# Two transformer blocks on one core: half of the modulation rows on GpSimd, reciprocal roots on VectorE

## The chip, the core and the metric

The kernel runs as one program on one core of a Trainium2 chip. The metric is the time of one execution on the device in microseconds (us). The kernel before was run three times: 1963.08 us in the median, 1960.91 to 1964.33.

The core has five instruction streams: TensorE (PE in the rows; its weight loads are PEld), VectorE (DVE), ScalarE (ACT), GpSimd (POOL) and SyncE (SP, which here only issues DMAs). Each takes its own instructions strictly in order, and an instruction that waits holds up all behind it on its engine.

## The reference

256 rows of 2048 numbers go through two blocks. The part that the change touches is cut out here:

```
c_act = silu(c)                                     # one row of 2048
for l in range(2):                                  # block 1, two layers
    mod = c_act @ w_mod[l] + b_mod[l]               # 2048 x 6144 weights
    shift, scale, gate = split(mod, 3)
    h = rmsnorm(x, g) * (1 + scale) + shift
    ... h @ w_in -> attention over 64 chosen keys, retention, head norms ...
    x = x + gate * (y @ w_out[l])
... block 2: h @ w_in, gated convolution, a gated recurrence, w_o, a gate, a last rmsnorm ...
rmsnorm(x, g) = x * rsqrt(mean(x * x) + 1e-6) * g
```

The modulation is a product of one row with a large matrix; `rsqrt` stands in every norm.

## The kernel before, in words

**Weight groups.** Almost all of TensorE's work is in `wgroup`: 512 columns of a weight for both halves of the rows. A weight comes in chunks of two row blocks (512 KB, tile `raw`, issued by SyncE at L226, three buffers). ScalarE rounds a chunk to `whi` (L231), VectorE takes the rest `wlo` (L233), and TensorE runs three products for each row block and half (L249, L250, L251): 12 matmuls a chunk.

**Modulation sums.** `gemv` holds a sum `acc` of 128 x 1024 over 16 rows of `w_mod` per partition. Each row is a 512 KB load into `graw` (L347, SyncE, three buffers), and VectorE multiplies it with a number of `ct` and adds it to `acc` (L351 for the first row, L353 for the others). TensorE then sums `acc` over partitions (L361 for shift and scale, L385 for the gate). There are 12 such sums, six a layer. The first one, at the start, is the wide one: it uses `raw` buffers too, and nothing else runs beside it.

**Order.** The sums are generators that run in the background of the weight groups: after each chunk `step()` advances every job by its rate (`RATE`, such as 0.902 rows a chunk for the first layer's rows). A scheduler then orders each engine's instructions by program order, moved by the places in `AHEAD` (`gdve` puts the sum's rows ten places later). Layer 0 goes over its first ten groups in four passes of 20 chunks, each pass with a quarter of the rows of the weight. A pass needs the normed rows of its quarter, and so the modulation sum of that quarter, which runs in the pass before it.

**Reciprocal roots.** `rstd` turns sums of squares into reciprocal roots for 1, 2 or 4 columns, on GpSimd: L152 scales and adds the epsilon, L154 takes the power -0.5, L156, L157, L158 and L160 are one Newton step. It runs 33 times. Its results go to `dg` (L517, VectorE, at the start), to `rq` (L616), `nm` (L780) and `ev` (L600, L1097) on VectorE, to the rows of the next layer (L912, ScalarE) and to the last norm (L1283, L1285, L1287).

Of the kernel before, what the change touches and what calls it, by code (L numbers as in the profile page):

```python
# [18 lines left out]
P = 128  # L19
# [8 lines left out]
# steps of each background job per weight chunk  # L28
# [3 lines left out]
# places that instructions move forward in the order of issue  # L32
# [3 lines left out]
WJ, NB = 12, 6  # L36
# [3 lines left out]
def shape_constants():  # L40
    """Tables that depend on shapes alone."""
# [27 lines left out]
def build(tc, a, out):  # L69
# [4 lines left out]
    with es:  # L74
# [5 lines left out]
        # ---------------------------------------------------------------- helpers  # L80
# [20 lines left out]
        def step(n=1):  # L101
            """Advance every background job by its rate."""
# [12 lines left out]
        def spawn(gen, rate, then=None):  # L115
            """Start a background job; another may follow it."""
            bg.append([gen, rate, 0.0, then])
# [10 lines left out]
        def give(consumer, t, pt):  # L128
            """Run a consumer up to its yield; what follows waits for flush()."""
            r = consumer(t, pt)  # L130
            if r is not None:
                next(r)
                late.append(r)
# [15 lines left out]
        def rstd(ss, n, mean):  # L149
            """(ss * mean + EPS) ** -0.5 for a [P, n] tile of sums of squares."""  # L150
            v = sm(n, "rv")
            G.tensor_scalar(v, ss, mean, EPS, op0=OP.mult, op1=OP.add)  # L152
            y = sm(n, "ry")
            G.tensor_tensor(y, v, mhalf[:, 0:n], op=OP.pow)  # L154
            q = sm(n, "rq")
            G.tensor_mul(q, y, y)  # L156
            G.tensor_mul(q, q, v)  # L157
            G.tensor_scalar(q, q, -0.5, 1.5, op0=OP.mult, op1=OP.add)  # L158
            z = sm(n, "rz")
            G.tensor_mul(z, y, q)  # L160
            return z
# [6 lines left out]
        def split_ps(ps, gain=None):  # L168
            """A [P, 512] transposed block in PSUM into its two float32r parts."""
# [36 lines left out]
        def build_kg(src, kg, gains, shifts):  # L206
            """One tile of four transposed blocks: normed rows scaled, shifted, split."""
# [9 lines left out]
        def build_raw(src, kg, gains):  # L217
            """Four transposed blocks of rows that are still to be normed, times the norm's gains."""
            return split_ps(transpose4(src), gains[:, kg * 4:kg * 4 + 4])

        def wchunk(srcs, n, kt):
            """Two row blocks of a weight, loaded and split."""
# [13 lines left out]
        def wgroup(srcs, n, aT, kts, consumer, mode="k", tw=3):  # L236
            """out[t] = rows[t] @ W for one group of columns; kts are row blocks (pairs from even)."""
# [41 lines left out]
        # ---------------------------------------------------------------- constants, small vectors  # L279
# [9 lines left out]
        mhalf = con.tile([P, 4], F32, name="mhalf")  # L289
        G.memset(mhalf, -0.5)  # L290
# [35 lines left out]
        # ---------------------------------------------------------------- modulation  # L326
# [6 lines left out]
        def gemv(l, ranges, wide=False):  # L333
            acc = b1.tile([P, 1024], F32, name="acc", tag="acc", bufs=2)
            for j in range(16):
# [13 lines left out]
                with tc.high_priority(offset=AHEAD["gdve"]):  # L349
                    if j == 0:  # L350
                        V.tensor_scalar(acc, rf, ct[:, 0:1], None, op0=OP.mult)  # L351
                    else:
                        last[0] = V.scalar_tensor_tensor(acc, rf, ct[:, j:j + 1], acc, op0=OP.mult, op1=OP.add)  # L353
# [22 lines left out]
        def mod_gate(l, q):  # L376
            """Half q of layer l's gate, on every partition."""
# [16 lines left out]
        # ---------------------------------------------------------------- T5 bias table, rotary tables  # L394
# [82 lines left out]
        # ---------------------------------------------------------------- start  # L477
# [75 lines left out]
        # ---------------------------------------------------------------- block 1  # L553
        def from_ps(pt, sb):
            """Columns in SBUF: as they are, or copied out of PSUM."""
# [6 lines left out]
        def layer(l, hT, ap):  # L562
# [62 lines left out]
            def select(t):  # L625
                """0 where a key is among the TOPK of its row and not after it, NEG elsewhere."""
# [726 lines left out]
```

## Time and profile before

| | |
|---|---|
| median of three runs | 1963.08 us |
| the profiled execution, first to last instruction | 1964.1 us |
| TensorE busy | 1849.0 us (94%) |
| VectorE busy | 1313.3 us (67%) |
| ScalarE busy | 1044.1 us (53%) |
| GpSimd busy | 93.0 us (5%) |
| granted TensorE clock, mean | 0.986 |

The profiled execution's own time is given as its span. A row of a timeline reads: start, duration, engine, line, operation, tile written and tiles read, shapes, count, and in brackets how long the engine had been idle before it and what ended that. In a group of instructions, busy time and mean duration stand behind the first bar and idle time before them behind the second. TensorE's busy time is modelled from pipelined matmuls, so that a busy TensorE need not be at its peak.

### The profile page before, as it was taken

How to read it: one execution, taken by the hardware profiler on the slowest of the kernel's cores; microseconds unless marked ns; L12 is line 12 of the kernel's file. 1: busy time of each engine (PE TensorE's matmuls, PEld its weight loads, DVE VectorE, ACT ScalarE, POOL GpSimd, SP SyncE). 2: the span in 40 equal slices, each digit the busy share in tenths (PEclk: the TensorE clock that was granted, in tenths of full speed). 3: DMA queues.
4: the chain of work that ended last, by engine and by line, in shares of the span. 5: the costliest groups of instructions: out<-in, count | busy, mean ns of one | idle time of the engine just before them, and what ended most of it. 6: DMA issues, size and time to landing. Idle time of an engine off the chain costs nothing.

```text
span 1964.1 us, 24148 instructions
## 1 busy us (share of the span) xinstructions
PE 1849.0 (94%) x8670; PEld 1503.6 (77%) x8670; DVE 1313.3 (67%) x1713; ACT 1044.1 (53%) x1576; POOL 93.0 (5%) x220
## 2 busy tenths in 40 slices
PE   3988899998997999999999999999999999999997
PEld 3866577777776877688878878888888888888786
DVE  6787669998777677976755565656575545455554
ACT  3557484554435455447545675458445444445554
POOL 2000011001101002100000100000000000000100
PEclk9999899999998999999999999999999999999999
DMA  9987777987888898875547765556656666657564
GB/s 316 327 269 251 249 234 224 320 293 235 295 300 264 295 309 282 269 223 157 163 156 239 214 181 174 151 171 183 177 151 191 194 193 193 193 183 222 176 205 146
DMA packets 230921, 440.37 MB, mean 224 GB/s; under 512 B 19728, under 2 KB 32144, under 8 KB 230672
## 3 DMA queue, kind: packets, MB, share of 16 engines
q1 hardware_dynamic: 228880, 436.38, 70.5%
q10 hardware_dynamic: 1440, 2.34, 0.3%
q8 instruction: 68, 1.11, 0.2%
q14 instruction: 53, 0.43, 0.1%
q0 software_dynamic: 480, 0.10, 0.0%
HBM read 430.85 MB, written 7.91 MB: 223 GB/s over the span
## 4 chain that ended last, share of the span: by engine, by line
PE 60%; DMA 15%; DVE 11%; ACT 5%; issue 5%; POOL 3%; SPq 1%; ACTq 0%; DVEq 0%; POOLq 0%
PE mm L250 18%; PE mm L251 18%; PE mm L249 18%; DMA graw<-in_w_mod_dram 8%; DVE wlo L233 5%; DMA raw<-in_w_in_dram 4%; DMA rb<-reld 2%; ACT whi L231 2%; DVE acc L353 2%; PE tr L196 2%; PE tr L1070 1%; POOL ry L154 1%; DVE I L648 1%; POOL rv L152 1%; SPq L226 1%
## 5 line engine op out<-in xcount | busy, mean ns | idle before, releaser
L233 DVE TENSOR_TENSOR wlo<-raw,whi 128x1024 fp32r<-128x1024 f32 (+1 forms) x596 | 721.6, 1213 | 409.5 <-ACT whi L231 407.8
L231 ACT CAST whi<-raw 128x1024 fp32r<-128x1024 f32 (+1 forms) x596 | 621.9, 1045 | 696.7 <-PE mm L251 451.3
L250 PE MATMUL mm<-wlo,ah 128*128 128x512 f32 (+1 forms) x2368 | 935.8, 395 | 23.5 <-DVE wlo L233 23.2
L249 PE MATMUL mm<-whi,ah 128*128 128x512 f32 (+1 forms) x2368 | 934.5, 397 | 11.8 <-ACT ah L187 7.7
L251 PE MATMUL mm<-whi,al 128*128 128x512 f32 (+1 forms) x2368 | 931.0, 393 | 0.7 <-DVE al L188 0.6
L250 PEld LDWEIGHTS mm<-wlo,ah 128*128 128x128 f32 x2368 | 449.0, 190 | 132.2 <-DVE wlo L233 44.6
L249 PEld LDWEIGHTS mm<-whi,ah 128*128 128x128 f32 x2368 | 447.7, 189 | 108.8 <-ACT ah L187 8.4
L251 PEld LDWEIGHTS mm<-whi,al 128*128 128x128 f32 x2368 | 448.5, 189 | 92.1 <-DVE al L188 2.2
L353 DVE SCALAR_TENSOR_TENSOR acc<-graw,ct,acc 128x1024 f32<-128x1024 f32 x174 | 223.0, 1282 | 63.4 <-DMA graw<-in_w_mod_dram 62.8
L851 DVE TENSOR_TENSOR sp<-sp,mm 128x512 f32<-128x512 f32 (+1 forms) x64 | 42.0, 660 | 15.1 <-PE mm L251 15.0
L196 PE MATMUL tr<-blob,ev 128*128 128x128 f32 x192 | 34.2, 277 | 5.2 <-DVE ev L737 4.1
L179 ACT ACTIVATE ev<-tr,vT 128x128 f32<-128x128 f32 x112 | 32.4, 378 | 9.9 <-PE tr L196 9.3
L481 ACT ACTIVATE junk<-xs 128x512 bf16<-128x512 f32 (+1 forms) x42 | 25.6, 610 | 21.5 <-DMA xs<-in_x_dram 9.4
L152 POOL TENSOR_SCALAR rv<-tot 128x1 f32<-128x1 f32 (+1 forms) x9 | 3.7, 413 | 652.9 <-DVE tot L203 639.6
L154 POOL TENSOR_TENSOR ry<-rv,mhalf 128x4 f32<-128x4 f32 (+2 forms) x33 | 34.2, 1036 | 2.8
L196 PEld LDWEIGHTS tr<-blob,ev 128*128 128x128 f32 x192 | 23.6, 140 | 13.5 <-issue 6.0
L196 PE MATMUL tr<-blob,xs 128*128 128x128 f32 x128 | 24.5, 285 | 8.8 <-ACT xs L912 6.3
L462 ACT ACTIVATE oh<-rb,blob 128x512 f32<-128x512 uint8 x24 | 16.2, 715 | 27.0 <-DMA rb<-reld 27.0
L1070 PEld LDWEIGHTS tr<-X 128*128 128x128 f32 x224 | 27.0, 192 | 2.0 <-ACT uT L1119 1.0
L1070 PE MATMUL tr<-X 128*128 128x128 f32 x224 | 27.5, 276 | 0.1
L196 PEld LDWEIGHTS tr<-blob,xs 128*128 128x128 f32 x128 | 16.8, 146 | 13.8 <-ACT xs L912 7.4
L469 PE MATMUL ms<-ohr,rb 128*32 128x512 f32 x48 | 16.0, 428 | 11.2 <-ACT ohr L465 11.1
(275 smaller groups left out, 1183.8 us busy)
## 6 DMA issues: line engine op xcount, KB each, us to landing
raw<-in_w_in_dram SPq DMA_DIRECT2D x416, 512.0 KB
graw<-in_w_mod_dram SPq DMA_DIRECT2D x186, 512.0 KB
raw<-in_w_out_dram SPq DMA_DIRECT2D x64, 512.0 KB
raw<-in_w_o_dram SPq DMA_DIRECT2D x32, 512.0 KB
raw<-in_w_ple_gate_dram SPq DMA_DIRECT2D x32, 512.0 KB
raw<-in_w_a_out_dram SPq DMA_DIRECT2D x16, 512.0 KB
raw<-in_w_b_out_dram SPq DMA_DIRECT2D x16, 512.0 KB
raw<-in_w_in_dram SPq DMA_DIRECT2D x16, 256.0 KB
```

The source lines that it names most:

```text
L154: G.tensor_tensor(y, v, mhalf[:, 0:n], op=OP.pow)
L179: A.activation(e[:, s], ps[:, s], AF.Copy, scale=gain[:, i:i + 1])
L196: T.transpose(ps[:, s], src[:, s], ident)
L231: A.copy(hi, raw)
L233: V.tensor_sub(lo, raw, hi.bitcast(F32))
L249: T.matmul(o, ah, hi[:, j, :], start=first, stop=False)
L250: T.matmul(o, ah, lo[:, j, :], start=False, stop=False)
L251: T.matmul(o, al, hi[:, j, :], start=False, stop=end)
L353: last[0] = V.scalar_tensor_tensor(acc, rf, ct[:, j:j + 1], acc, op0=OP.mult, op1=OP.add)
L481: A.activation(junk[:, :n], src, AF.Square, accum_out=acc)
L851: V.tensor_add(h, h, pt[:, :n])
L1070: T.matmul(ps[:, h * P:(h + 1) * P], X[:, h, s], X[:, h, s], start=True, stop=True)
```

## The change

In every sum but the first, rows 8 to 15 go to GpSimd, as two instructions: the row is multiplied in its own buffer, and then added to `acc`. `NV = 8` is the row from which that holds. The reciprocal roots go to VectorE: an integer shift and subtraction on the bits of the number give a first guess, and three Newton steps of three instructions follow, 12 instructions in all in place of six. The tile `mhalf` goes. Loads, rates and places are as they were. Below, comments that were taken out and line moves are left out.

```diff
-WJ, NB = 12, 6
+WJ, NB, NV = 12, 6, 8
...
         def rstd(ss, n, mean):
             v = sm(n, "rv")
-            G.tensor_scalar(v, ss, mean, EPS, op0=OP.mult, op1=OP.add)
+            V.tensor_scalar(v, ss, mean, EPS, op0=OP.mult, op1=OP.add)
             y = sm(n, "ry")
-            G.tensor_tensor(y, v, mhalf[:, 0:n], op=OP.pow)
-            q = sm(n, "rq")
-            G.tensor_mul(q, y, y)
-            G.tensor_mul(q, q, v)
-            G.tensor_scalar(q, q, -0.5, 1.5, op0=OP.mult, op1=OP.add)
-            z = sm(n, "rz")
-            G.tensor_mul(z, y, q)
-            return z
+            V.tensor_scalar(y.bitcast(I32), v.bitcast(I32), 1, None, op0=OP.logical_shift_right)
+            V.tensor_scalar(y.bitcast(I32), y.bitcast(I32), -1.0, 1597463007.0, op0=OP.mult, op1=OP.add)
+            for _ in range(3):
+                q = sm(n, "rq")
+                V.scalar_tensor_tensor(q, y, -0.5, y, op0=OP.mult, op1=OP.mult)
+                V.tensor_mul(q, q, v)
+                z = sm(n, "rz")
+                V.scalar_tensor_tensor(z, q, 1.5, y, op0=OP.add, op1=OP.mult)
+                y = z
+            return y
...
                     if j == 0:
                         V.tensor_scalar(acc, rf, ct[:, 0:1], None, op0=OP.mult)
+                    elif wide or j < NV:
+                        last[0] = V.scalar_tensor_tensor(acc, rf, ct[:, j:j + 1], acc, op0=OP.mult, op1=OP.add)
                     else:
-                        last[0] = V.scalar_tensor_tensor(acc, rf, ct[:, j:j + 1], acc, op0=OP.mult, op1=OP.add)
+                        G.tensor_scalar(rf, rf, ct[:, j:j + 1], None, op0=OP.mult)
+                        last[0] = G.tensor_add(acc, acc, rf)
```

VectorE at the start, before the change: `tot` is the sum of squares of the input rows, `dg` the diagonal matrix with the reciprocal roots, and each `acc` a row of the first sum.

```order
L353 SCALAR_TENSOR_TENSOR acc<-raw,ct,acc 128x1024
L511 TENSOR_REDUCE tot<-sqx 128x2
L353 SCALAR_TENSOR_TENSOR acc<-graw,ct,acc 128x1024
L517 TENSOR_SCALAR dg<-blob,rz 128x128 x2
L353 SCALAR_TENSOR_TENSOR acc<-raw,ct,acc 128x1024
L353 SCALAR_TENSOR_TENSOR acc<-graw,ct,acc 128x1024
L353 SCALAR_TENSOR_TENSOR acc<-raw,ct,acc 128x1024
L353 SCALAR_TENSOR_TENSOR acc<-graw,ct,acc 128x1024 x4
```

The same place of the changed kernel, from the second `acc` behind `tot` on (`tot`, two steps, an `acc` and three more steps stand ahead of it).

```order
L355 SCALAR_TENSOR_TENSOR acc<-raw,ct,acc 128x1024
L162 SCALAR_TENSOR_TENSOR rz<-rq,ry 128x2
L159 SCALAR_TENSOR_TENSOR rq<-rz 128x2
L160 TENSOR_TENSOR rq<-rq,rv 128x2
L355 SCALAR_TENSOR_TENSOR acc<-graw,ct,acc 128x1024
L162 SCALAR_TENSOR_TENSOR rz<-rq,rz 128x2
L159 SCALAR_TENSOR_TENSOR rq<-rz 128x2
L160 TENSOR_TENSOR rq<-rq,rv 128x2
L355 SCALAR_TENSOR_TENSOR acc<-raw,ct,acc 128x1024
L162 SCALAR_TENSOR_TENSOR rz<-rq,rz 128x2
L522 TENSOR_SCALAR dg<-blob,rz 128x128 x2
L355 SCALAR_TENSOR_TENSOR acc<-graw,ct,acc 128x1024 x4
```

The steps of the reciprocal root stand between rows of the sum, and `dg` stands behind four rows of the sum where it stood behind one.

VectorE in the second half of the second sum, in layer 0's first pass, changed kernel: `wlo` is a weight chunk's rest, `Sh` what reads TensorE's sum of `acc`.

```order
L355 SCALAR_TENSOR_TENSOR acc<-graw,ct,acc 128x1024
L236 TENSOR_TENSOR wlo<-raw,whi 128x672
L355 SCALAR_TENSOR_TENSOR acc<-graw,ct,acc 128x1024
L236 TENSOR_TENSOR wlo<-raw,whi 128x1024 x2
L355 SCALAR_TENSOR_TENSOR acc<-graw,ct,acc 128x1024
L236 TENSOR_TENSOR wlo<-raw,whi 128x1024 x12
L368 TENSOR_TENSOR Sh_77<-tr,vT 128x4
```

Before, an `acc` stood between nearly every two of those last twelve; they are now on GpSimd, whose rows there are these (numbers tell the buffers apart).

```order
L357 TENSOR_SCALAR graw_521<-graw_521,ct_66 128x1024
L358 TENSOR_TENSOR acc_306<-acc_306,graw_521 128x1024
L357 TENSOR_SCALAR graw_543<-graw_543,ct_66 128x1024
L358 TENSOR_TENSOR acc_306<-acc_306,graw_543 128x1024
L357 TENSOR_SCALAR graw_571<-graw_571,ct_66 128x1024
L358 TENSOR_TENSOR acc_306<-acc_306,graw_571 128x1024
```

TensorE's sums of `acc` keep their places in its order in layer 0: behind chunk 18, 38 and 58 in both kernels.

VectorE where layer 0 ends, changed kernel: `tot` is the sum of squares of the new rows' first half, `xs` those rows.

```order
L206 TENSOR_REDUCE tot<-ssx 128x1
L355 SCALAR_TENSOR_TENSOR acc<-graw,ct,acc 128x1024
L236 TENSOR_TENSOR wlo<-raw,whi 128x1024 x2
L153 TENSOR_SCALAR rv<-tot 128x1
L892 TENSOR_TENSOR xs<-mm,gate 128x512
L155 TENSOR_SCALAR ry<-rv 128x1
L355 SCALAR_TENSOR_TENSOR acc<-graw,ct,acc 128x1024
L156 TENSOR_SCALAR ry<-ry 128x1
L159 SCALAR_TENSOR_TENSOR rq<-ry 128x1
L160 TENSOR_TENSOR rq<-rq,rv 128x1
```

Before, the same `acc`, `wlo`, `xs` and `acc` followed `tot`, but the reciprocal root ran beside them on GpSimd.

## Rows read from the trace of the kernel before

**Rows 1.** The page: span, and busy time of each engine.

```profile
span 1964.1 us, 24148 instructions
PE 1849.0 (94%) x8670; PEld 1503.6 (77%) x8670; DVE 1313.3 (67%) x1713; ACT 1044.1 (53%) x1576; POOL 93.0 (5%) x220
```

**Rows 2.** Busy time by stage: us; PE, PEld, DVE, ACT, POOL; clock, DMA, GB/s.

```profile
45.00:98.00 53.00, 53.00 (x244) 44.20 (x244) 41.32 (x42) 29.28 (x42) 0.00 (x0) 0.98 0.97 329
98.00:295.00 197.00, 171.35 (x744) 127.96 (x743) 141.34 (x182) 128.66 (x218) 9.14 (x22) 0.95 0.78 250
295.00:835.00 540.00, 502.67 (x2380) 401.30 (x2380) 437.96 (x627) 267.25 (x447) 41.66 (x89) 0.98 0.85 281
835.00:1964.00 1129.00, 1108.34 (x5220) 917.67 (x5219) 666.26 (x829) 601.10 (x837) 31.30 (x84) 0.99 0.61 184
```

**Rows 3.** The page's groups: weight rests, their matmuls, the sums' rows.

```profile
L233 DVE TENSOR_TENSOR wlo<-raw,whi 128x1024 fp32r<-128x1024 f32 (+1 forms) x596 | 721.6, 1213 | 409.5 <-ACT whi L231 407.8
L250 PE MATMUL mm<-wlo,ah 128*128 128x512 f32 (+1 forms) x2368 | 935.8, 395 | 23.5 <-DVE wlo L233 23.2
L353 DVE SCALAR_TENSOR_TENSOR acc<-graw,ct,acc 128x1024 f32<-128x1024 f32 x174 | 223.0, 1282 | 63.4 <-DMA graw<-in_w_mod_dram 62.8
```

**Rows 4.** Timeline at the start: the diagonal, the transposes, the first sum's matmuls.

```profile
26.47 0.48 DVE L517 TENSOR_SCALAR dg<-blob,rz 128x128 f32<-128x128 f32 x2 [2.00 <-POOL rz L160]
26.81 9.14 PE L198 MATMUL tr<-dg,xs 128*128 128x128 f32 x64 [11.09 <-DVE dg L517]
37.55 0.69 PE L361 MATMUL tr<-blob,acc 128*128 128x1 f32 x5 [1.60 <-DVE rbd L441]
```

**Rows 5.** Timeline: GpSimd instructions that begin beside a VectorE instruction, in pairs.

```profile
105.36 1.27 DVE L353 SCALAR_TENSOR_TENSOR acc<-graw,ct,acc 128x1024 f32<-128x1024 f32 x1
105.52 1.59 POOL L415 TENSOR_TENSOR tmp<-pti,tmp 128x256 int32<-128x256 int32 x1 [0.90 <-DVE tmp L417]
...
301.38 1.28 DVE L353 SCALAR_TENSOR_TENSOR acc<-graw,ct,acc 128x1024 f32<-128x1024 f32 x1
301.52 1.46 POOL L152 TENSOR_SCALAR rv<-ssq 128x4 f32<-128x4 f32 x1 [4.83 <-ACT junk L481]
```

**Rows 6.** Timeline: a VectorE instruction that begins beside a GpSimd one.

```profile
294.51 1.01 POOL L154 TENSOR_TENSOR ry<-rv,mhalf 128x4 f32<-128x4 f32 x1
294.55 1.23 DVE L233 TENSOR_TENSOR wlo<-raw,whi 128x1024 fp32r<-128x1024 f32 x1
```

**Rows 7.** Timeline: second sum's row 8; TensorE at the second and fourth sums' ends.

```profile
69.38 1.28 DVE L353 SCALAR_TENSOR_TENSOR acc<-graw,ct,acc 128x1024 f32<-128x1024 f32 x1
...
92.78 1.84 PE L361 MATMUL tr<-blob,acc 128*128 128x1 f32 x16
...
245.44 1.80 PE L361 MATMUL tr<-blob,acc 128*128 128x1 f32 x15 [1.17 <-DVE acc L353]
```

**Rows 8.** Timeline where layer 0 ends.

```profile
589.90 0.15 DVE L203 TENSOR_REDUCE tot<-ssx 128x1 f32<-128x4 f32 x1
593.61 0.69 DVE L887 TENSOR_TENSOR xs<-mm,gate 128x512 f32<-128x512 f32 x1
594.10 0.19 POOL L160 TENSOR_TENSOR rz<-ry,rq 128x1 f32<-128x1 f32 x1
595.10 1.97 PE L196 MATMUL tr<-blob,xs 128*128 128x128 f32 x8 [4.80 <-ACT xs L912]
```

**Rows 9.** VectorE's smallest operation by form, and waits for reciprocal roots (us, times, longest).

```profile
L366 DVE SCALAR_TENSOR_TENSOR Gm<-mq,vT 128x4 f32<-128x4 f32 x8 | 1.3, 160 | 0.1
DVE nm L780 <- POOL rz L160: 13.2, 8, 2.3
DVE ev L1097 <- POOL rz L160: 12.7, 4, 3.6
DVE rq L616 <- POOL rz L160: 10.2, 7, 2.3
```

**Rows 10.** Timeline at the end: the last norm's first use.

```profile
1958.08 0.49 DVE L1285 TENSOR_SCALAR xs<-xs,rz 128x512 f32<-128x512 f32 x1 [2.04 <-POOL rz L160]
```

More of the change, by code (lines that the diff above doesn't have):

```diff
@@ L287, in build @@
         lev = con.tile([P, 7, P], U8, name="lev")
-        mhalf = con.tile([P, 4], F32, name="mhalf")
-        G.memset(mhalf, -0.5)
         vT = con.tile([P, 128], F32, name="vT")
```

## The prediction

> **What bounds the kernel now.** The page says TensorE first: it is busy for 1849.0 of 1964.1 us [rows 1]. The table by stage then says where it is not. From 835 us on it idles for 20.7 of 1129 us, so nothing that the change does to another engine can be worth much there. Before that it idles for 62.98 us (25.65 from 98 to 295, 37.33 from 295 to 835), in stages where the DMAs are busy for 0.78 to 0.97 of the time and VectorE for 620.6 of 790 us [rows 2]. All 12 modulation sums lie in this first part. The groups say how VectorE and TensorE meet there: the second of a chunk's three matmuls idles for 23.5 us in all, almost only for `wlo`, and the sums' rows keep VectorE for 223.0 us and leave it idle for 63.4 us more while it waits, in order, for their loads [rows 3]. So the change can win at most about what TensorE waits for `wlo`, and can lose wherever a sum or a reciprocal root that TensorE waits for comes later.
>
> **The rows that go to GpSimd.** 11 sums by 8 rows: 88 multiply-adds of 1.282 us leave VectorE, 112.8 us, and with them about half of the 63.4 us of waiting in its queue [rows 3]. In place of each GpSimd runs two instructions over 1024 columns. The trace has none so wide. The widest on GpSimd is the int32 subtraction of 256 columns: it began at 105.52, beside a VectorE row of a sum that ended at 106.63, and ended at 107.11, 0.48 us later [rows 5]. By columns that is 1.92 us for 1024, 3.8 us for a row of a sum, and this I take. From below: the 4-column `rv` ended 0.32 us after the VectorE instruction beside it (301.38 + 1.28 to 302.98), so 252 more columns cost 0.16 us, and 1024 columns 0.32 + 0.65 = 0.97 us, 1.9 a row. From above: the whole 1.59 us as GpSimd's own price is 6.4 us, 12.7 a row. The nearest row is the subtraction's own part.
>
> *Does GpSimd run beside VectorE?* Both pairs of [rows 5] say that it waits: a 4-column `rv` lasts 1.46 us when it begins 0.14 us into a sum's row, and the end of that row ends it. The other way round, `wlo` began 0.04 us into a GpSimd power of 1.01 us and took 1.23, against 1.213 on average [rows 3, 6]; but that power reads four columns. The Trainium skill (SBUF — State Buffer, Who interferes with whom) says that a VectorE instruction with two SBUF inputs and a GpSimd instruction that reads SBUF share a port as an exclusive lock, held by whichever began first for its whole length. The rows agree for the one direction; no row here shows it for the other, which would speak against this change. The skill's GPSIMD Engine Reference (Elementwise — side-by-side cycle accounting) gives 4497 ns for an addition of 2048 columns; an estimate from that page is 2.25 us for 1024, which would make the row 4.2 us in place of 3.8.
>
> *The second sum.* Layer 0's first pass is bound by TensorE (53.00 of 53 us [rows 2]). 244 matmuls at 12 a chunk are 20.3 chunks, 2.6 us each. Row 8 was added at 69.38; the new order lets SyncE issue its load two chunks earlier, so GpSimd can begin near 64.2, and eight rows of 3.8 us end at 94.6. TensorE came to the sum at 92.78 without idle time [rows 7]: +2 us. With rows of 1.9 us it is 0; with two waits of 1.22 us for `wlo` in each row (6.2 us) it is +21 us. Behind the waiting matmul stand the whole next pass, and on VectorE `Sh` and all that follows it.
>
> *The fourth sum.* There TensorE already idles for 1.17 us for the last row [rows 7]. A last row of 3.8 us in place of 1.28 adds 2.5 us (0.6 to 5). The third sum's rows came 4 us apart and the later sums end well ahead of their matmuls: 0.
>
> *What VectorE loses.* If GpSimd's instructions also hold VectorE, 88 rows of 3.8 us are 334 us. VectorE's slack in 45 to 835 is 790 - 620.6 = 169 us, and 112.8 are freed: 52 us too much is the upper end. The lower end is 0, as in [rows 6]. I take 6, near the row, since that row is of a short reader.
>
> *What TensorE gains.* Of its 23.5 us for `wlo` all could go at best; GpSimd rows are under half of all rows of the sums, so I take -10.
>
> **The reciprocal roots.** 12 instructions of 0.16 us [rows 9] are 1.9 us, as long as VectorE's wait for GpSimd at the end (2.04 [rows 10]): the end costs 0. 33 times 12 are 396 instructions or 63 us of VectorE, and 36.1 us of waits for `rz` go [rows 9]: 27 us more, spread over stages where VectorE has 632 us to spare: 0, covered by that slack; without it a few us (bounds -4 and +5).
>
> Two places lose, because a chain that ran beside VectorE's queue now stands in it. *Start:* `dg` moves behind three more rows of the first sum (3 x 1.28) and 12 steps (1.9), and the 2.00 us of waiting goes: +3.8 us. The transposes then end at 26.81 + 9.14 + 3.8 = 39.75, and with ScalarE's last copy of some 0.6 the sum's matmuls begin at 40.35, not 37.55: +2.8 us (1 to 5) [rows 4]. *End of layer 0:* from `tot` (589.90) to `rz` (594.29) it took GpSimd 4.4 us, and TensorE idled for 4.80 us for what follows. Now an `acc` (1.28), two `wlo` (2.4), `xs` (0.69), another `acc` (1.28) and 12 steps (1.9) stand in VectorE's queue ahead of the result: 7.6 us, +3.2 (0 to 3.5) [rows 3, 8].
>
> **Sum.** +2.8 + 2 + 2.5 + 3.2 + 6 - 10 = +6.5 on the profiled span of 1964.1, so 1970.6; that span lies 1.0 above the median of the runs, which makes the forecast 1970 us.
>
> **Rivals.**
> *Relief wins.* VectorE no longer stands waiting for half of the loads, `wlo` comes in time, and SyncE gets `raw` buffers back sooner. For it: the 63.4 us of waits in VectorE's own queue, and 23.5 on TensorE. Against it: the DMAs are at 0.85 and more in those stages already. With all of the 23.5, no holding of VectorE, short GpSimd rows (second sum 0, fourth +0.6) and the two lost places (+6): -17, 1946 us. It decides where GpSimd's row stays under the 2.6 to 4 us in which rows arrive.
>
> *They cancel.* Relief of 15, VectorE not held, the sums' ends as forecast: +2.8 + 2 + 2.5 + 3.2 - 15 = -4.5, or somewhat less relief: 1963 us.
>
> *The two engines take turns.* A GpSimd instruction holds VectorE as VectorE holds GpSimd. Place: rows 8 to 15 of each sum. Price: a GpSimd row takes 6.2 us, the second sum ends 21 us late, and `wlo` is held for some of the 52 us. With half of that: +2.8 + 21 + 5 + 3.2 + 26 - 10 = +48, less what the loads gain while TensorE stands, say 15: 1996 us. It decides when a GpSimd row takes more than 4 us. The Trainium skill's exclusive lock (SBUF — State Buffer) would do this.
>
> **Chances.** Slower as forecast 0.31, taking turns 0.12, relief 0.36, cancelling 0.21. 0.2% of 1963 us, 3.9 us, is what a measurement tells from no change: faster by more 0.36, within 0.21, slower by more 0.43. The likeliest case alone runs from 1965 to 1982. The range for 8 in 10 goes from 1943 to 1997: from all of the relief to the turns.
>
> **What would show it.** GpSimd's busy time by its two new lines: near 88 x 3.8 = 334 us. TensorE's idle time before the second and the fourth sum's matmuls: 2 and 3.7 us. `dg` near 30 us, the first weight matmul near 46 in place of 43.3. The mean `wlo` beside GpSimd rows: 1.21 if it isn't held, above 1.5 if it is. TensorE's wait for `wlo`: 13 us in place of 23. I am wrong if GpSimd's row takes under 2.5 us, or if the `wlo` waits vanish whole.

## The result, and the profile after

The changed kernel took 2148.65 us (median of 4 runs, 2144.98 to 2156.88), the kernel before 1962.24 us (4 runs, 1960.91 to 1964.33): a ratio of 1.0955, 95% interval 1.093 to 1.098. The forecast of 1970 us, range 1943 to 1997, was far too low: the sign was right, the size was not.

The page of the changed kernel, to be held against [rows 1]:

```profile
span 2143.2 us, 24433 instructions
PE 1897.2 (89%) x8670; PEld 1539.3 (72%) x8670; DVE 1375.0 (64%) x2021; ACT 1044.7 (49%) x1576; POOL 529.1 (25%) x197
...
PE 57%; POOL 17%; DMA 9%; DVE 9%; issue 3%; ACT 3%; SPq 0%; ACTq 0%; DVEq 0%; POOLq 0%
```

The third line is the chain of work that ended last. GpSimd, busy for a quarter of the time, is 17% of it, some 364 us. Before the change it was 3%:

```profile
PE 60%; DMA 15%; DVE 11%; ACT 5%; issue 5%; POOL 3%; SPq 1%; ACTq 0%; DVEq 0%; POOLq 0%
```

The span is 179.1 us longer: TensorE idles for 246.0 us in place of 115.1 (span less busy), and is busy for 48.2 us more with the same 8670 matmuls. The table by stage (us; PE, PEld, DVE, ACT, POOL; clock, DMA, GB/s) says where, with the stages of [rows 2] moved by the delay:

```profile
45.00:112.00 67.00, 53.73 (x216) 42.51 (x216) 34.62 (x30) 28.99 (x41) 44.07 (x15) 0.88 0.73 245
112.00:350.00 238.00, 185.13 (x784) 139.54 (x785) 136.31 (x207) 133.04 (x228) 97.08 (x36) 0.90 0.66 214
350.00:1010.00 660.00, 532.44 (x2346) 423.65 (x2345) 492.20 (x750) 265.25 (x440) 379.98 (x128) 0.90 0.70 229
1010.00:2143.00 1133.00, 1113.84 (x5245) 922.47 (x5243) 684.91 (x989) 602.16 (x839) 0.00 (x0) 0.99 0.61 183
```

The last stage, without sums, takes 1133 us against 1129 before. All the rest arises where the sums are. There the DMAs, at 0.78 to 0.97 before, are down to 0.66 to 0.73, and the mean granted clock is 0.88 to 0.90 (a mean over TensorE's two levels, 1.2 and 2.4 GHz) in place of 0.95 to 0.98: the 48.2 us more of "busy" are matmuls at the lower level, in stretches with gaps. Less traffic and more idle time fit weights that come late.

The groups that answer to [rows 3], the two new GpSimd lines, and the matmuls at the sums' ends:

```profile
L236 DVE TENSOR_TENSOR wlo<-raw,whi 128x1024 fp32r<-128x1024 f32 (+1 forms) x596 | 764.1, 1284 | 503.3 <-ACT whi L234 501.6
L253 PE MATMUL mm<-wlo,ah 128*128 128x512 f32 (+1 forms) x2368 | 947.7, 400 | 51.2 <-DVE wlo L236 51.0
L357 POOL TENSOR_SCALAR graw<-graw,ct 128x1024 f32<-128x1024 f32 x88 | 298.8, 3396 | 385.8 <-DMA graw<-in_w_mod_dram 217.9
L358 POOL TENSOR_TENSOR acc<-acc,graw 128x1024 f32<-128x1024 f32 x88 | 222.7, 2530 | 32.2 <-DVE acc L355 25.0
L355 DVE SCALAR_TENSOR_TENSOR acc<-graw,ct,acc 128x1024 f32<-128x1024 f32 x86 | 118.8, 1382 | 39.5 <-DMA graw<-in_w_mod_dram 38.9
L366 PE MATMUL tr<-blob,acc 128*128 128x1 f32 x128 | 21.4, 297 | 33.5 <-POOL acc L358 33.5
```

A GpSimd row is 3.40 + 2.53 = 5.9 us, not 3.8. VectorE's `wlo` went from 1.213 to 1.284 us, and TensorE's wait for it from 23.2 to 51.0 us. But these waits do not add up to 131 us. The missing view is SyncE's own queue, whose waits nothing counts as busy (us in all, times, longest):

```profile
SPq L229 <- DVE wlo L236: 1036.6, 455, 13.6
SPq L349 <- POOL acc L358: 285.1, 68, 7.5
```

The first is the normal state of a queue that runs ahead until a weight buffer comes free (1104.3 us before the change). The second is new. Before the change SyncE waited for VectorE's rows, for 58.4 us in all and never longer than 3.8:

```profile
SPq L347 <- DVE acc L353: 58.4, 49, 3.8
```

How the two meet is seen in the second half of the second sum. GpSimd's timeline (start, us, and so on):

```profile
84.55 2.41 POOL L358 TENSOR_TENSOR acc<-acc,graw 128x1024 f32<-128x1024 f32 x1
86.94 3.91 POOL L357 TENSOR_SCALAR graw<-graw,ct 128x1024 f32<-128x1024 f32 x1
90.94 2.35 POOL L358 TENSOR_TENSOR acc<-acc,graw 128x1024 f32<-128x1024 f32 x1
93.26 3.82 POOL L357 TENSOR_SCALAR graw<-graw,ct 128x1024 f32<-128x1024 f32 x1
97.16 2.35 POOL L358 TENSOR_TENSOR acc<-acc,graw 128x1024 f32<-128x1024 f32 x1
```

and SyncE's:

```profile
86.99 0.37 SPq L349 DMA_DIRECT2D graw<-in_w_mod_dram  x1
87.46 0.41 SPq L229 DMA_DIRECT2D raw<-in_w_in_dram  x1
93.31 0.37 SPq L349 DMA_DIRECT2D graw<-in_w_mod_dram  x1
93.77 0.42 SPq L229 DMA_DIRECT2D raw<-in_w_in_dram  x1
99.54 0.37 SPq L349 DMA_DIRECT2D graw<-in_w_mod_dram  x1
```

GpSimd's addition ends at 86.96, and at 86.99 SyncE issues the load into the buffer that this frees; only then, in order, the load of one weight chunk at 87.46. The next pair comes with the next addition, 6.3 us later. The weight buffer had long been free: with three buffers, the chunk three places earlier had to be done, and VectorE's `wlo` of that one ended at 81.75. TensorE then waited 2.16 us for the chunk that was loaded at 87.46:

```profile
79.59 2.16 DVE L236 TENSOR_TENSOR wlo<-raw,whi 128x1024 fp32r<-128x1024 f32 x1 [2.06 <-ACT whi L234]
...
93.14 0.50 PE L252 MATMUL mm<-whi,ah 128*128 128x512 f32 x1 [2.16 <-ACT whi L234]
```

Before the change TensorE used up a chunk in 2.6 us; from 81 to 100 us it now gets one for each of GpSimd's rows.

### The profile page after: what moved, and what is told of

It is laid out like the page before. It is cut to its first block, busy times and chain, and to the rows that moved or that the text cites. A ratio compares the mean times of both kernels' runs of the same rounds, so it can differ in the third digit from the quotient of the medians.

```text
span 2143.2 us, 24433 instructions
## 1 busy us (share of the span) xinstructions
PE 1897.2 (89%) x8670; PEld 1539.3 (72%) x8670; DVE 1375.0 (64%) x2021; ACT 1044.7 (49%) x1576; POOL 529.1 (25%) x197
## 3 DMA queue, kind: packets, MB, share of 16 engines
q10 hardware_dynamic: 1440, 2.34, 0.3%
## 4 chain that ended last, share of the span: by engine, by line
PE 57%; POOL 17%; DMA 9%; DVE 9%; issue 3%; ACT 3%; SPq 0%; ACTq 0%; DVEq 0%; POOLq 0%
PE mm L253 17%; PE mm L254 17%; PE mm L252 17%; POOL graw L357 10%; POOL acc L358 7%; DMA graw<-in_w_mod_dram 5%; DVE wlo L236 3%; DVE acc L355 1%; DMA raw<-in_w_out_dram 1%; PE tr L199 1%; PE tr L1075 1%; ACT whi L234 1%; DMA raw<-in_w_in_dram 1%; DVE I L653 1%; PE tr L366 1%
## 5 line engine op out<-in xcount | busy, mean ns | idle before, releaser
L236 DVE TENSOR_TENSOR wlo<-raw,whi 128x1024 fp32r<-128x1024 f32 (+1 forms) x596 | 764.1, 1284 | 503.3 <-ACT whi L234 501.6
L253 PE MATMUL mm<-wlo,ah 128*128 128x512 f32 (+1 forms) x2368 | 947.7, 400 | 51.2 <-DVE wlo L236 51.0
L252 PE MATMUL mm<-whi,ah 128*128 128x512 f32 (+1 forms) x2368 | 949.9, 403 | 22.4 <-ACT whi L234 14.0
L254 PE MATMUL mm<-whi,al 128*128 128x512 f32 (+1 forms) x2368 | 941.4, 398 | 11.0 <-DVE al L191 10.9
L254 PEld LDWEIGHTS mm<-whi,al 128*128 128x128 f32 x2368 | 455.5, 192 | 106.1 <-DVE al L191 13.3
L357 POOL TENSOR_SCALAR graw<-graw,ct 128x1024 f32<-128x1024 f32 x88 | 298.8, 3396 | 385.8 <-DMA graw<-in_w_mod_dram 217.9
L358 POOL TENSOR_TENSOR acc<-acc,graw 128x1024 f32<-128x1024 f32 x88 | 222.7, 2530 | 32.2 <-DVE acc L355 25.0
L355 DVE SCALAR_TENSOR_TENSOR acc<-graw,ct,acc 128x1024 f32<-128x1024 f32 x86 | 118.8, 1382 | 39.5 <-DMA graw<-in_w_mod_dram 38.9
L366 PE MATMUL tr<-blob,acc 128*128 128x1 f32 x128 | 21.4, 297 | 33.5 <-POOL acc L358 33.5
L366 PEld LDWEIGHTS tr<-blob,acc 128*128 128x128 f32 x128 | 21.4, 258 | 35.4 <-POOL acc L358 35.0
L182 ACT ACTIVATE ev<-tr,vT 128x128 f32<-128x128 f32 x112 | 32.7, 375 | 13.4 <-PE tr L199 10.9
L653 DVE SCALAR_TENSOR_TENSOR I<-sc,wi,I 128x128 f32<-128x128 f32 (+1 forms) x60 | 36.2, 604 | 0.5
L353 DVE TENSOR_SCALAR acc<-graw,ct 128x1024 f32<-128x1024 f32 x12 | 16.0, 1332 | 30.7 <-DMA graw<-in_w_mod_dram 30.7
```

What stands on the lines that cost most here:

```text
L236: V.tensor_sub(lo, raw, hi.bitcast(F32))
L252: T.matmul(o, ah, hi[:, j, :], start=first, stop=False)
L253: T.matmul(o, ah, lo[:, j, :], start=False, stop=False)
L254: T.matmul(o, al, hi[:, j, :], start=False, stop=end)
L357: G.tensor_scalar(rf, rf, ct[:, j:j + 1], None, op0=OP.mult)
L358: last[0] = G.tensor_add(acc, acc, rf)
```

## The experiments

All times are medians of 4 to 10 runs, beside runs of the kernel before of 1964.36 to 1965.91 us. The two theories through most of them: *pace* (SyncE stops for GpSimd's buffers, with the weights behind), and *hold* (GpSimd's instructions keep VectorE's waiting).

**The two halves of the change.** The roots alone:

```diff
-WJ, NB, NV = 12, 6, 8
+WJ, NB, NV = 12, 6, 16
```

> All rows of the sums on VectorE again, reciprocal roots on VectorE as in the changed kernel. Theory P (the pace of a GpSimd row, 5.9 us against the 3 to 5 us in which rows come, is what costs: it keeps the three row buffers, SyncE waits for them, and the weights behind them come late): the 186 us go, and what is left is the two places named in the prediction, +6 us: 1968 us (1962 to 1974). Theory R (the 12 steps in VectorE's queue cost): over 2000 us.

Measured: 1976.01 us, ratio 1.006 (1.0046 to 1.0075). The rows alone, with the roots of before:

```diff
-            V.tensor_scalar(v, ss, mean, EPS, op0=OP.mult, op1=OP.add)
+            G.tensor_scalar(v, ss, mean, EPS, op0=OP.mult, op1=OP.add)
             y = sm(n, "ry")
+            G.tensor_tensor(y, v, mhalf[:, 0:n], op=OP.pow)
...
```

> Half of the rows on GpSimd, reciprocal roots on GpSimd as before the change. Theory P: the loss stays, and the roots now queue behind rows of 5.9 us: 2140 to 2200 us. Theory R: most of the loss goes, under 2000 us.

Measured: 2152.23 us, 1.0955 (1.0928 to 1.0982). The rows are all of the loss; the roots cost 12 us alone and can't be seen beside the rows.

**Which of the roots.** VectorE keeps the roots of four columns; those of one or two go back to GpSimd:

```diff
         def rstd(ss, n, mean):
+            if n < 4:
+                v = sm(n, "rv")
+                G.tensor_scalar(v, ss, mean, EPS, op0=OP.mult, op1=OP.add)
+                y = sm(n, "ry")
+                G.tensor_tensor(y, v, mhalf[:, 0:n], op=OP.pow)
...
+                return z
             v = sm(n, "rv")
...
```

> All rows on VectorE, and of the roots only those of four columns (the heads' norms) on VectorE; those of one or two columns (the rows' norms, at the start and at the ends of the layers, and the key's) on GpSimd as before. Theory P (the 12 us that the roots alone cost arise where a row's root stands between two products with nothing to cover it, and VectorE works off its twelve small instructions among long ones): 1955-1968 us. Rival Q (they arise at the heads' roots, which make the block's streams of long VectorE work later): 1970-1980 us.

Measured: 1964.03 us, 0.9992 (0.9971 to 1.0013): no change from before. The 12 us of the roots are those of the rows' norms (and the key's, which went back with them). The heads' roots cost nothing on VectorE and win nothing: TensorE waits 10.9 us for `wlo` there in place of 23.2, and the time is the same.

**Does GpSimd hold VectorE?** All rows are on VectorE, and GpSimd does idle work (its result is read by nothing) over constants beside each of rows 8 to 15, paced by a one-column copy:

```diff
-WJ, NB, NV = 12, 6, 8
+WJ, NB, NV = 12, 6, 16
...
-                q = sm(n, "rq")
+                q = sm(n, "rq", 2)
...
+                        if not wide and j >= 8:
+                            go = wp.tile([P, 1], F32, name="go", tag="go", bufs=6)
+                            V.tensor_copy(go, acc[:, 0:1])
+                            tw = lev.rearrange("p a b -> p (a b)").bitcast(BF)
+                            for _ in range(2):
+                                G.tensor_scalar(tw, blob[:, 0:448], go, None, op0=OP.mult)
+                            for _ in range(2):
+                                G.tensor_add(tw, blob[:, 0:448], blob[:, 0:448])
```

> All rows of the sums on VectorE, roots on VectorE. After each of rows 8 to 15 VectorE copies one column, and that lets GpSimd run two multiplications and two additions of 448 columns over constants into a scratch tile that nothing reads: GpSimd is as busy as in the changed kernel, some 400 to 500 us, but no load, no sum and no matmul waits for it. Theory P: within 15 us of the kernel with the roots alone. Theory H: 60 us or more above it, with weight rests of over 1.25 us on average beside GpSimd's work.

Measured: 2041.78 us, 1.0386 (1.0365 to 1.0407). The control has 8 columns in place of 448:

```diff
-                                G.tensor_scalar(tw, blob[:, 0:448], go, None, op0=OP.mult)
+                                G.tensor_scalar(tw[:, 0:8], blob[:, 0:8], go, None, op0=OP.mult)
...
-                                G.tensor_add(tw, blob[:, 0:448], blob[:, 0:448])
+                                G.tensor_add(tw[:, 0:8], blob[:, 0:8], blob[:, 0:8])
```

> The control to the run in which VectorE adds all rows and GpSimd runs four instructions over 448 columns beside each of rows 8 to 15 (2042 us): the same instructions on GpSimd in the same number, over 8 columns, with the same one-column copy on VectorE that paces them. Theory P (long instructions on GpSimd delay VectorE's): within 8 us of the roots alone, 1970-1984 us. Rival C (the copies on VectorE and what waits for GpSimd's queue cost it, the columns nothing): above 2025 us.

Measured: 1971.1 us, 1.0027 (1.0005 to 1.005). So 71 us come from the length of GpSimd's instructions alone, 66 against the roots alone. Not all of that is the hold. An instruction of the kernel's own on GpSimd (`tmp`, the int32 subtraction of [rows 5]) stood there behind the idle work, and VectorE waited 15.5 us for it, which it does not in the control:

```profile
DVE tmp L430 <- POOL tmp L428: 15.5, 1, 15.5
```

Behind that TensorE stood still for 15.7 us. That leaves some 50 to 55 us for the hold, an estimate (66 and 71, less 15.7). `wlo` and GpSimd's lines, with the idle work:

```profile
L236 DVE TENSOR_TENSOR wlo<-raw,whi 128x1024 fp32r<-128x1024 f32 (+1 forms) x596 | 760.6, 1279 | 393.3 <-ACT whi L234 392.1
L361 POOL TENSOR_SCALAR lev<-blob,go 128x448 bf16<-128x448 f32 x176 | 366.6, 2083 | 286.2 <-DVE go L358 258.3
L363 POOL TENSOR_TENSOR lev<-blob 128x448 bf16<-128x448 f32 x176 | 231.4, 1315 | 14.2
```

and `wlo` in the control:

```profile
L236 DVE TENSOR_TENSOR wlo<-raw,whi 128x1024 fp32r<-128x1024 f32 (+1 forms) x596 | 721.2, 1212 | 408.1 <-ACT whi L234 406.9
```

The hold is real: 1.279 against 1.212 us.

**Which of GpSimd's two instructions?** Only the additions, then only the multiplications:

```diff
-                        G.tensor_scalar(rf, rf, ct[:, j:j + 1], None, op0=OP.mult)
                         last[0] = G.tensor_add(acc, acc, rf)
```

> Leaves out the multiplication of rows 8 to 15 by their numbers, so the sums aren't those of the reference; GpSimd only adds, 2.5 us a row in place of 5.9. Theory P: the row is now faster than rows arrive, so nearly all of the loss goes: 1965 to 1990 us, and SyncE's waits for GpSimd fall from 285 us to under 60. Theory H (GpSimd's instructions hold VectorE, and its late weight rests are the loss): what is left goes by GpSimd's busy time, 223 of 522 us: about 80 of the 186 us, 2040 us.

Measured: 2034.13 us, 1.0353 (1.0335 to 1.0371), 58 us above the roots alone. That is the hold's number (2040), though SyncE's waits for GpSimd fell to 39.7 us, as the pace theory had them. The sums end on GpSimd here too, but TensorE waits only 3.7 us for these ends. The mean `wlo` is 1.289 us.

```diff
                         G.tensor_scalar(rf, rf, ct[:, j:j + 1], None, op0=OP.mult)
-                        last[0] = G.tensor_add(acc, acc, rf)
```

> The changed kernel without GpSimd's additions: it multiplies rows 8 to 15 and the products are left out of the sums, which end with VectorE's row 7. A GpSimd row is 2.8 to 3.4 us, about that of the run with the additions alone (2034 us). Theory P (what holds VectorE is the instruction with two inputs, the addition: in the changed kernel a wlo beside multiplications alone has a mean of 1.39 us, beside both 1.90; and three microseconds a row is faster than the rows came before): 1975-2000 us. Rival H (any long GpSimd instruction over 1024 columns holds VectorE alike): 2025-2045 us.

Measured: 1970.81 us, 1.003 (1.001 to 1.0049). GpSimd is busy for longer than with the additions (272.8 against 246.8 us in its one line), and the time is 5 us below the roots alone. That is a little under both ranges, on the side of the first. So GpSimd's busy time is not what costs. And 88 rows less on VectorE, 112.8 us of its work, are worth 5 us here, net of a slight hold (`wlo` 1.230 us, 1.214 with the roots alone); the intervals of the two ratios touch.

**How many rows.** Four rows of each sum on GpSimd:

```diff
-WJ, NB, NV = 12, 6, 8
+WJ, NB, NV = 12, 6, 12
```

> The changed kernel with only the last four rows of each half-width sum on GpSimd (44 rows in place of 88). Theory P (each GpSimd row has its price): half of the 172 us that eight rows cost over the roots alone (1976 us): 2045-2080 us. Rival T (up to three row buffers ahead, four rows pile up little, the cost is in the queue that eight rows in succession make): 1985-2015 us.

Measured: 2068.3 us, 1.0525 (1.0486 to 1.0564): 92 us over the roots alone, where eight rows cost 172. In proportion; three buffers hide little.

**The rows spread out.** As many GpSimd rows, but every other one, into a sum of their own:

```diff
-                    elif wide or j < NV:
+                    elif wide or j % 2 == 0:
...
+                    elif j == 1:
+                        ac2 = b1.tile([P, 1024], F32, name="acc", tag="acc", bufs=2)
+                        G.tensor_scalar(ac2, rf, ct[:, 1:2], None, op0=OP.mult)
...
-                        last[0] = G.tensor_add(acc, acc, rf)
+                        G.tensor_add(ac2, ac2, rf)
+                    if j == 15 and not wide:
+                        last[0] = V.tensor_add(acc, acc, ac2)
```

> The changed kernel, with GpSimd's eight rows of each half-width sum spread over it: rows 1, 3, ..., 15 on GpSimd into a sum of its own (the other of the two acc buffers), the even rows on VectorE, and one more VectorE addition of the two sums at the end. As many GpSimd rows as in the change, with two rows' time for each. Theory P (pace: the last eight rows in a row can't come faster than GpSimd's 5.9 us each, 47 us, where they took 22 to 47 us before, and the loads of the weights stand behind them in SyncE's order; the rest is VectorE's delay): the pace stops binding, some 100 us come back, 2030-2065 us. Rival E (each GpSimd row costs the same wherever it stands, by delaying VectorE and by its buffer): 2130-2160 us.

Measured: 2094.36 us, 1.0675 (1.0631 to 1.0718). 54 us come back, half of what the pace theory had; neither number was met. SyncE's waits for GpSimd fall from 285 to 139 us (two lines of 126.1 and 13.3), and the hold stays. GpSimd also waits here for the second `acc` buffer (170.0 us for TensorE to have read it), so the run isn't pure.

**The loads on GpSimd's own queue.**

```diff
-                    last[1] = Y.dma_start(dst, src)
+                    last[1] = (Y if wide or j < NV else G).dma_start(dst, src)
```

> The changed kernel, with the loads of the rows that GpSimd multiplies (rows 8 to 15 of each half-width sum) issued by GpSimd on its own queue, so that no DMA issue of SyncE waits for a buffer that GpSimd holds. Theory P (a GpSimd row costs three things: it delays VectorE's long instructions, worth about 66 us by the run with all rows on VectorE and idle work on GpSimd; it makes SyncE wait for the row's buffer with the weight loads queued behind; and it makes TensorE wait 33 us at the ends of sums): the second part goes, and the time falls from 2148 us to 2070-2110 us. Rival H (VectorE's delay and the late sums make up everything, SyncE's 285 us of waiting for GpSimd's adds is spare time of a queue that runs ahead): 2135-2160 us. Rival S (GpSimd's own issue comes too late behind its row work, so the sums end still later): above 2160 us.

Measured: 2164.42 us, 1.1015 (1.099 to 1.1041), the number of rival S. It tells less than it was meant to. SyncE still waits for GpSimd, since the loads of rows 0 to 7 use the same three buffers; and one wait was put in the place of another:

```profile
SPq L349 <- POOL acc L358: 174.6, 25, 23.2
...
L349 POOL DMA_DIRECT2D graw<-in_w_mod_dram x88 | 61.0, 693 | 356.8 <-DVE acc L355 215.9
L366 PE MATMUL tr<-blob,acc 128*128 128x1 f32 x128 | 20.1, 287 | 55.3 <-POOL acc L358 53.8
```

GpSimd's queue, in order too, now stands at the issue of a load until VectorE frees the buffer (215.9 us), and the sums end later still (53.8 us on TensorE). What the pace costs, this run does not show.

**A shorter row.** The multiplication as an instruction of two inputs:

```diff
-                        G.tensor_scalar(rf, rf, ct[:, j:j + 1], None, op0=OP.mult)
+                        G.tensor_tensor(rf, rf, ct[:, j:j + 1].to_broadcast([P, 1024]), op=OP.mult)
```

> The changed kernel with GpSimd's multiplication as an instruction of two inputs, the row and the factor read again and again for 1024 columns. Theory P (the pace of a GpSimd row sets the second half of the sums; by the addition's 2.5 us a row would be 5.0 in place of 5.9 us, 88 x 0.9 = 79 us, less some more delay of VectorE): 2080-2125 us. Rival H (VectorE's delay counts more than the pace, and the multiplication now delays it like the addition): 2140-2200 us.

Measured: 2141.27 us, 1.0911 (1.0883 to 1.0938), in the range of rival H and above that of the pace. The row fell to 5.2 us (2.352 + 2.859) and SyncE's wait for its buffer from 285.1 to 157.4 us, but the mean `wlo` rose to 1.368 us and TensorE's wait for it from 51.0 to 75.0 us. That the hold took what the pace gave would fit; no run parts the two here. What SyncE waits is not, us for us, what is lost.

**The pace without the additions.** Two multiplications a row and no addition, so that the buffer is kept as long as in the change, but no sum waits for GpSimd:

```diff
                         G.tensor_scalar(rf, rf, ct[:, j:j + 1], None, op0=OP.mult)
-                        last[0] = G.tensor_add(acc, acc, rf)
+                        G.tensor_scalar(rf, rf, ct[:, j:j + 1], None, op0=OP.mult)
```

> The changed kernel with two multiplications of each of GpSimd's rows and no addition (the products are left out of the sums, which end with VectorE's row 7). GpSimd is busy for some 6.2 us a row, a little over the 5.9 us of the change, and gives the row's buffer back as late, but no instruction of two inputs runs on it and no sum waits for it. Theory P (the pace of the rows reaches the weight loads through SyncE's order, and counts beside the delay of VectorE): 2025-2070 us, against 1971 us with one multiplication a row. Rival A (what costs time is the addition alone, by holding VectorE and by ending the sums late; SyncE's wait for a row's buffer is covered): 1968-1985 us.

Measured: 2106.24 us, 1.0721 (1.0684 to 1.0758): 135 us above one multiplication a row, more than the pace theory had (its range ended at 2070), and the rival is out. The chain that ended last, and the page's groups:

```profile
PE 56%; POOL 17%; DMA 12%; DVE 8%; issue 4%; ACT 3%; SPq 0%; ACTq 0%; POOLq 0%; DVEq 0%
...
L236 DVE TENSOR_TENSOR wlo<-raw,whi 128x1024 fp32r<-128x1024 f32 (+1 forms) x596 | 743.6, 1249 | 549.7 <-ACT whi L234 546.1
L357 POOL TENSOR_SCALAR graw<-graw,ct 128x1024 f32<-128x1024 f32 x88 | 269.4, 3062 | 364.5 <-DMA graw<-in_w_mod_dram 246.6
L358 POOL TENSOR_SCALAR graw<-graw,ct 128x1024 f32<-128x1024 f32 x88 | 267.3, 3038 | 8.2
```

SyncE's wait for a row's buffer there:

```profile
SPq L349 <- POOL graw L358: 340.8, 76, 8.5
```

and with one multiplication a row:

```profile
PE 66%; DMA 13%; DVE 10%; ACT 5%; issue 3%; SPq 1%; POOL 1%; ACTq 0%; DVEq 0%; POOLq 0%
...
L357 POOL TENSOR_SCALAR graw<-graw,ct 128x1024 f32<-128x1024 f32 x88 | 272.8, 3110 | 465.5 <-DMA graw<-in_w_mod_dram 323.4
```

with SyncE's wait:

```profile
SPq L349 <- POOL graw L357: 63.4, 29, 5.8
```

At 3.1 us a row SyncE waits 63 us for GpSimd and nothing is lost; at 6.1 us it waits 341 us and 135 are lost. No sum takes GpSimd's products in these runs, so its two instructions stand in the chain (17%, against 1%) by the buffers that they give back: followed in order of time, each of the ten stretches of GpSimd's rows in it is released into a load. The second multiplication also adds some hold, but too little to be the loss: `wlo` takes 21 us more in all than with the roots alone (743.6 against 722.4), where the additions alone add 45 (766.9) and cost 58.

**The late ends.** The same, and one more multiplication of each sum on GpSimd, meant to stand behind its eight rows:

```diff
+                        if j == 15:
+                            last[0] = G.tensor_scalar(acc, acc, ones[:, 0:1], None, op0=OP.mult)
```

> The same two multiplications a row and no addition, and after row 15 one more multiplication of the sum itself by one on GpSimd, so that each sum ends on GpSimd behind its eight rows as in the change, again without an instruction of two inputs. Theory P (the ends of the sums on GpSimd cost TensorE what it waited there in the change, 33 us, and what that brings behind it): 30 to 60 us above the run without that instruction. Rival A (the sums' ends have time to spare, the waits only take the place of others): within 12 us of it.

Measured: 2123.93 us, 1.08 (1.0762 to 1.0837): 18 us more, between the two expectations. But the run is not what it was meant to be. The sum needs nothing of rows 8 to 15 here, and in GpSimd's order the new instruction stands ahead of them in nearly every sum (behind all eight in one of eleven). In the second:

```profile
65.57 3.75 POOL L360 TENSOR_SCALAR acc<-acc,blob 128x1024 f32<-128x1024 f32 x1 [26.34 <-DVE acc L355]
69.31 2.84 POOL L357 TENSOR_SCALAR graw<-graw,ct 128x1024 f32<-128x1024 f32 x1
```

So the sums do not end behind GpSimd's rows, and TensorE waits only 1.5 us for them. Beside the 18 us stand GpSimd's 36 us more of work and 187.6 us in which its queue waits there for VectorE's row 7. What the late ends of the change cost, beyond the 33.5 us that TensorE waits for them, no run shows.

**The account**, from one run to the next: before 1964; the roots +12 (1976); 88 rows off VectorE and multiplied on GpSimd -5 (1971); a row's time doubled +135 (2106); the addition in place of the second multiplication, with sums that end on GpSimd, +42 (2149). The last step holds the addition's hold and the late ends together (the chain of the changed kernel leaves GpSimd's rows three times into a sum's matmuls, from the second sum to the fourth, and six times into a load), and is smaller than the 58 us that additions cost alone or the 50 to 55 left of the idle work. That holding VectorE costs less while it waits for late weights anyway would fit, but no run shows it.

No version here beats both kernels: the nearest, with the heads' roots on VectorE, ties with before.

## Why the prediction was wrong

*What bounds the kernel* was read rightly: nothing is lost after the last sum, and the sums' stages lose whatever comes late.

*The step that failed* stands at the end of the fourth sum: "The third sum's rows came 4 us apart and the later sums end well ahead of their matmuls: 0." I asked of each sum only whether TensorE would stand waiting for its end. I did not ask who waits for a row's buffer. By the kernel's order SyncE issues the loads of rows and weights in one queue, with three row buffers; a GpSimd row that lasts longer than the gap between rows (5.9 us against 2.6 to 4) stops that queue, and every weight chunk behind it. Nine of the eleven sums were priced at nothing, and the 135 us of the pace stood in no term. My rival on the relief had the right condition (a GpSimd row under "the 2.6 to 4 us in which rows arrive"): the run at 3.1 us a row lies inside and lost nothing, the one at 6.1 us lies above. But for being above nothing was charged except the second and the fourth sum's ends and the hold.

*The row's price* pushed it above that. The 0.48 us by which an int32 subtraction of 256 columns outlasted VectorE's row [rows 5] scaled to 1.92 us for 1024. That remainder was not its own price: the same subtraction took 0.61 us in the run with each sum's extra multiplication, 2.4 by columns. Undisturbed, the addition takes 2.34 us (the shortest of 88) and the multiplication 2.84: 5.2 us, and 5.9 on average with the turns. I had taken an instruction of one input as no dearer than one of two. It is dearer. My upper bound of 12.7 us a row held it, but the range was built with 6.2 us in one case of 0.12. GpSimd's two lines were busy for 521.5 us, not near 334.

*The sums' ends.* Forecast: TensorE idles for 2 us before the second sum, 0 before the third, 3.7 before the fourth. Answering to [rows 7]:

```profile
116.03 3.57 PE L366 MATMUL tr<-blob,acc 128*128 128x1 f32 x16 [9.92 <-POOL acc L358]
...
204.49 3.57 PE L366 MATMUL tr<-blob,acc 128*128 128x1 f32 x16 [13.80 <-POOL acc L358]
...
298.42 3.58 PE L366 MATMUL tr<-blob,acc 128*128 128x1 f32 x16 [9.73 <-POOL acc L358]
```

TensorE comes to the second sum 23 us late (116.03 against 92.78), near the +21 of my upper bound, 6.2 us a row, behind the late start of some 3 us. That is in part luck: the bound was made of 3.8 us and two waits of 1.22, the measured row of 5.2 and some 0.7 of waiting. The third sum, which I had at 0, makes TensorE wait longest, 13.80 us.

*VectorE held by GpSimd:* +6 was taken, of 0 to 52; the idle work showed some 50 to 55 us, near the upper end, though with GpSimd busy for 598 us in place of the 334 behind that bound. The row that I leaned on, a `wlo` beside a four-column power, was too short a reader, as the prediction itself noted. The test that it named came out for the hold: 47 `wlo` of the changed kernel that lie beside both of GpSimd's instructions have a mean of 1.90 us, those beside none 1.21 (my mean over the records).

*The rival in which the engines take turns* named the hold, its place and a row's price of 6.2 us. Its 1996 us was low because it, too, charged the second and the fourth sum alone and half of the hold, and no stopped queue. Two slips beside it: the sum of the rival that cancels, -4.5, gives 1959 and not 1963, and the DMAs, said to be at 0.85 and more, were at 0.78 from 98 to 295 us [rows 2].

*The relief of `wlo`*, -10: 88 rows off VectorE were worth 5 us where a GpSimd row took 3.1 us. In the change TensorE's wait went to 51.0 us, not to 13.

*The start* was right: `dg` +4.1 us (30.53, forecast +3.8), the sum's matmuls at 40.89 (40.35), the first weight matmul at 46.7 (near 46). *The end of layer 0* was right too, read in the run of the roots alone, against [rows 8]:

```profile
599.31 0.15 DVE L206 TENSOR_REDUCE tot<-ssx 128x1 f32<-128x4 f32 x1
...
607.14 0.16 DVE L162 SCALAR_TENSOR_TENSOR rz<-rq,rz 128x1 f32<-128x1 f32 x1
...
608.11 1.97 PE L199 MATMUL tr<-blob,xs 128*128 128x128 f32 x8 [7.86 <-ACT xs L917]
```

From `tot` to `rz` 8.0 us (7.6 forecast), and TensorE idles for 7.86 us in place of 4.80: +3.1 (3.2). Yet the roots cost 12 us in all, twice these two terms; where the other 6 arise among the rows' roots wasn't followed.

## What to carry to other kernels

Before work moves to a slower engine, compare the new time of one step with the gap between steps, and then look at who waits for the step's buffer: if its loads share an in-order queue with the loads that feed the bounding engine, a step that is too slow stops those as well, and the price is counted per step and not at the end of the sum. The bounding engine's list of waits hides this, because what it then waits for carries the names of its usual feeders; the DMA queue's own waits show it. And 113 us of work taken off an engine that is 67% busy were worth some 5 us, where nothing else was lost by it.

## What the runs showed of the hardware

A multiplication of 128x1024 f32 by a factor for each partition takes GpSimd 2.84 us at the least, longer than an addition of two such tiles (2.34).

The turns are exact. GpSimd's timeline in the changed kernel:

```profile
384.13 5.61 POOL L358 TENSOR_TENSOR acc<-acc,graw 128x1024 f32<-128x1024 f32 x2 [24.98 <-DVE acc L355]
389.72 3.82 POOL L357 TENSOR_SCALAR graw<-graw,ct 128x1024 f32<-128x1024 f32 x1
```

and VectorE's:

```profile
387.42 3.40 DVE L236 TENSOR_TENSOR wlo<-raw,whi 128x1024 fp32r<-128x1024 f32 x1
```

The `wlo` begins beside an addition that ends at 389.74, and ends 1.08 us after that: it waited for the whole addition. The multiplication that follows takes 3.82 in place of 2.84 us, since it waited for the `wlo`. In the run of additions alone 34 of the 39 `wlo` that began inside an addition ended 1.08 to 1.09 us after its end.

Multiplications hold less. GpSimd's timeline in the run with them alone:

```profile
507.62 5.67 POOL L357 TENSOR_SCALAR graw<-graw,ct 128x1024 f32<-128x1024 f32 x2
```

and VectorE's:

```profile
509.14 1.22 DVE L236 TENSOR_TENSOR wlo<-raw,whi 128x1024 fp32r<-128x1024 f32 x1
510.55 2.08 DVE L236 TENSOR_TENSOR wlo<-raw,whi 128x1024 fp32r<-128x1024 f32 x1
```

The first `wlo` begins 1.52 us into a multiplication and takes its 1.22; the second begins 0.12 us into the next (at 510.44) and takes 2.08, ending 0.66 us before that multiplication does. All that began within the first 0.7 us of an undisturbed multiplication ended 0.65 to 0.66 us ahead of its end, so VectorE is kept out for about the first 0.97 us of 2.84 (2.84 less 0.66 and the `wlo`'s own 1.21, an estimate). The Trainium skill (SBUF — State Buffer, Who interferes with whom) states a lock for the whole length of the instruction; the trace agrees for the additions (and for `wlo` holding GpSimd), and not for the multiplications.
